# A two-layer hybrid block on one core: strands for casts, subtractions and sums of weights; modulation buffers; new planner costs

## The chip, the cores and the metric

One NeuronCore of one Trainium2 chip runs the whole computation in one launch. The metric is the device time of that launch in microseconds. The engines are called as in the profile: PE (TensorE matmul), PEld (its weight load), DVE (VectorE), ACT (ScalarE), POOL (GpSimd) and SP (SyncE, which here only issues DMAs).

## The reference, cut to what matters

Everything is float32. There are 512 latent tokens and 256 context tokens of 1024 features, and two layers. The context's stream ends inside layer 1, so layer 0 works on 768 tokens and layer 1 on 512 (and on the context's keys and values).

```python
m = silu(cvec) @ w_ada + b_ada                  # 6 x 1024 modulation values, for c and for c_ctx
h = rmsnorm(x, g1) * (1 + sc1) + sh1
z = h @ w_in                                    # 1024 -> 2304: gMLP, gated conv, 2-D Fourier, attention
mix = concat(mixer_a(z), mixer_b(z), mixer_c(z), diff_attention(z))
x = x + gt1 * (mix @ w_out)
h2 = rmsnorm(x, g2) * (1 + sc2) + sh2
up = h2 @ w_up                                  # 1024 -> 2 x 2816
x = x + gt2 * ((silu(dwconv3(up[:2816])) * up[2816:]) @ w_down)
```

The modulation `m` is needed in pieces: `sh1, sc1` before a layer's first projection, `gt2` only when the down projection's results are scaled.

## The kernel before, in words

**Operands.** Features lie on the partitions and tokens on the free axis. A float32 operand is split into a high part (rounded to fp32r by a cast) and a low part (the difference), and each product takes three matmul passes: high by high, high by low, low by high. A weight tile of 128x1024 is loaded into a `wr` buffer by a DMA of SP's queue (4 such buffers), ACT casts it to `wh`, and DVE or POOL subtracts it to `wl` (5 buffers of each). Such a pair is called a unit; the list `plan` fixes their order for the whole program. `load_units` issues the loads, `split_units` makes the units.

**FFN.** The up projection goes by 22 rows f of 128 hidden features, each with an `a` and a `b` half. The first four rows (PLAIN) are plain products with `h2`. From f = 4 on, two rows are taken together as a "quad": seven products on half the tokens in place of eight. For the left factors `split_quad` needs two loaded tiles r0 and r1 and a third buffer rs, four sums of weight pieces (`wr<-wr` on DVE) and four units (.0, .1, .2 of full and .3, `s4h`/`s4l`, of half width). For the right factors `right_factors` builds sums of `h2` blocks once a layer; a last step of it (`hhi<-t`, `hlo<-t`) overwrites halves of `h2`, and can run only when the plain rows have been read. Rows are grouped in chunks (FFN_CHUNKS); the down projection of one chunk comes on PE after the up projection of the next. Each of its eight outputs is scaled by `gt2` on ACT (`ev<-banks,ada`, one instruction a token group) and added to DRAM by a DMA of POOL's queue (`xacc<-ev`); the last chunk alone is added on chip.

**Modulation.** Layer 0's first 40 blocks are made on PE at the start. The other 8 (the `gt2` of layer 0) and the 48 of layer 1 are made by `next_ada` on DVE: one block is a 512 KB load `adaw` by SP's queue and one or two multiply-accumulate instructions over 1024 elements (two where the context needs its own value: blocks 40 to 47 of layer 0 and 0 to 15 of layer 1), then a small add of the bias. It starts when layer 0's mid norm is done. Its two buffers of the pool AR serve for the loaded block and, with two instructions, for the unused product of the first (`junk`).

**The order.** The program is written out by a planner (`Sched`) while it is built. Strands (Python generators) offer instructions; the planner keeps a clock per engine, assumes a duration for each instruction, and always emits the strand that can start first; among those that can start at once it takes the smallest priority number, then the strand that was spawned first. The order in which instructions are emitted is the order in which each engine runs them, and on the chip they wait for one another by semaphores alone. So the assumed durations decide only the order, and the choice of the engine where an instruction may go to several (`("dve", "pool")`). `wl_engine` forces subtractions to POOL in the norm stages and in part of attention. Posts (what follows a product) have priority 1, `split_units` 2, `load_units` 3, `next_ada` 5.

**Lines.** L216 is every plain matmul, L258 every cast or copy on ACT, L261 a copy on DVE, L268 and L270 every two-input elementwise operation on DVE and on POOL, L282 every DVE instruction with a scalar and two tensors, L295 and L297 a scaling on ACT and on POOL, L198 the adding DMA, L189 every other DMA.

Of the kernel before, what the change touches and what calls it, by code (L numbers as in the profile page):

```python
# [29 lines left out]
FFN_CHUNKS = [2] * 9 + [4]  # L30
# [20 lines left out]
SEM = 0.16  # L51
PEM = 0.08
# [25 lines left out]
TAB = 1.1  # L78


class Sched:
# [7 lines left out]
    BW = 320  # L89

    def __init__(self, nc):
        self.nc = nc
        self.T = dict(pe=0.0, act=0.0, dve=0.0, pool=0.0, sp=0.0)
        self.dclk = 0.0
        self.now = 0.0
# [30 lines left out]
    def _ready(self, req):  # L126
        if callable(req):
            return req()
        opts, outs, ins = req
        return min(max(self._deps(o[0], outs, ins) + (PEM if o[0] == "pe" else 0.0), self.T[o[0]]) for o in opts)  # L130

# [28 lines left out]
    def op(self, opts, outs, ins):  # L160

        yield opts, outs, ins
        start = {o[0]: max(self.T[o[0]], self._deps(o[0], outs, ins)) for o in opts}
# [6 lines left out]
        self.T[e] = end  # L170
        self.busy[e] = self.busy.get(e, 0) + cost
# [7 lines left out]
    def dma(self, out, in_, queues=("sp",)):  # L179
        nc = self.nc  # L180
        eng = dict(sp=nc.sync, act=nc.scalar, pool=nc.gpsimd)
        cost = dict(sp=0.6, act=0.7, pool=1.05)
# [4 lines left out]
        for d in sb[0].shape:  # L187
            n *= d
        yield from self.op([(q, cost[q], lambda q=q: eng[q].dma_start(out, in_)) for q in queues], outs, ins)  # L189
        self.dclk = max(self.dclk, self.now) + 4 * n / self.BW / 1e3  # L190
        for o in outs:
            self._note(self.W, o, self.dclk + 2.2, "dma")
        for i in ins:
            self.R[i.tensor.name].append((*span(i)[1:], self.dclk + 2.2, "dma"))

    def dma_add(self, out, in_):

        yield from self.op([("pool", 1.05, lambda: self.nc.gpsimd.dma_start(out, in_, accum_op=ALU.add))], [], [in_])  # L198
# [3 lines left out]
        self.dclk = max(self.dclk, self.now) + 8 * n / self.BW / 1e3  # L202
        self.R[in_.tensor.name].append((*span(in_)[1:], self.dclk + 2.2, "dma"))
# [22 lines left out]
    def trs(self, items, ident):  # L226
# [3 lines left out]
        yield from self.op([("pe", 0.109 * len(items), emit)], [i[0] for i in items], [i[1] for i in items])  # L230

    def _act(self, out, in_, func, bias=None, scale=1.0, accum=None):
        k = {}
        ins = [in_]
        cost = 0.19 + self.n(in_) / 1200
        for key, v in (("bias", bias), ("scale", scale)):
# [3 lines left out]
            if not isinstance(v, float):  # L240
                ins.append(v)
                cost += 0.09
        outs = [out]
        if accum is not None:
            k["accum_out"] = accum
            outs.append(accum)
            cost += 0.28
# [6 lines left out]
    def copy(self, out, in_, eng=("act",)):  # L254
# [4 lines left out]
        if "dve" in eng:  # L259
            fast = in_.space != bass.MemoryType.PSUM  # L260
            opts.append(("dve", 0.09 + n / (1920 if fast else 960), lambda: self.nc.vector.tensor_copy(out, in_)))  # L261
        yield from self.op(opts, [out], [in_])

    def tt(self, out, a, b, op, eng=("dve",)):
        n = self.n(out)
        opts = []
        if "dve" in eng:
            opts.append(("dve", 0.09 + n / 960, lambda: self.nc.vector.tensor_tensor(out, a, b, op=op)))  # L268
# [4 lines left out]
        yield from self.op(opts, [out], [a, b])  # L273
# [1529 lines left out]
```

## Time and profile before

| | |
|---|---|
| three runs | 1571.81, 1567.7, 1562.89 us, median 1567.7 |
| profiled execution, its own time | 1568.05 us |
| its span, first to last instruction | 1566.3 us |
| PE busy | 1457.6 us (93%) |
| DVE busy | 1172.2 us (75%) |
| ACT busy | 751.5 us (48%) |
| POOL busy | 380.6 us (24%) |
| mean granted PE clock | 0.975 |

The stages, by the span's clock: the start and layer 0's projections and mixers to about 350 us, its norms to 400, its FFN to about 890; layer 1's norm and mixers to about 1165, its FFN to about 1530, then the final norm. Busy time of an engine is read beside what ended its idle time: an engine that is 75% busy can still be what PE waits for.

### The profile page before, as it was taken

Reading aid. Unit: us, or ns where it says so; the run is one execution under the profiler, and the core shown is the slowest. Engines: PE = TensorE matmul, PEld = TensorE weight load, DVE = VectorE, ACT = ScalarE, POOL = GpSimd, SP = SyncE. Lnnn points to the kernel's source line nnn. Section 1 sums busy time; section 2 is a strip of 40 time slices with the busy share of each in tenths; the row PEclk is TensorE's granted clock in tenths of the full one; section 3 lists DMA queues with packets and bytes.
Section 4 is the critical chain, followed back from the end, with each engine's and each line's share of the span. In section 5 each row is a group of like instructions: output and inputs, shape, how many; then the busy total and the mean of one; then the engine's idle time right before and its main releaser. Section 6 shows DMA issues by size and latency. Waiting matters only on the chain.

```text
span 1566.3 us, 24259 instructions
## 1 busy us (share of the span) xinstructions
PE 1457.6 (93%) x9312; PEld 1287.5 (82%) x9312; DVE 1172.2 (75%) x1924; ACT 751.5 (48%) x1161; POOL 380.6 (24%) x368
## 2 busy tenths in 40 slices
PE   6989999997979999999999979978989899999987
PEld 4877787886869999999999869766878788888877
DVE  4748578658977777787869487879778777777785
ACT  4435455223535455555445344735334565555552
POOL 0202422107111112211111323343054222222212
PEclk9999999999989999999999989999999999999999
DMA  9564433115165677665566756253441676665635
GB/s 374 155 210 167 135 91 115 41 54 175 54 150 130 179 185 191 150 165 145 150 185 193 215 184 189 101 153 137 141 135 43 147 157 145 163 155 135 153 111 154
DMA packets 79444, 235.45 MB, mean 150 GB/s; under 512 B 10912, under 2 KB 13088, under 8 KB 79200
## 3 DMA queue, kind: packets, MB, share of 16 engines
q1 hardware_dynamic: 50304, 160.72, 30.9%
q0 software_dynamic: 27872, 72.01, 22.2%
q8 instruction: 73, 1.20, 0.3%
q10 hardware_dynamic: 1152, 1.18, 0.2%
q14 instruction: 43, 0.35, 0.1%
HBM read 165.70 MB, written 56.62 MB: 142 GB/s over the span
## 4 chain that ended last, share of the span: by engine, by line
PE 59%; DVE 24%; issue 6%; DMA 5%; ACT 4%; POOL 2%; SPq 0%; DVEq 0%; ACTq 0%; POOLq 0%
PE banks L216 57%; DVE wl L268 4%; DVE hlo L282 2%; DVE wr L268 2%; DVE mx L308 2%; ACT wh L258 1%; DVE ss L268 1%; DVE fy L282 1%; DVE ht L282 1%; DMA stk<-rhi 1%; DVE adaw L282 1%; PE banks L229 1%; DMA adaw<-in_w_adaT 1%; DVE p L282 1%; DVE lo L268 1%
## 5 line engine op out<-in xcount | busy, mean ns | idle before, releaser
L216 PE MATMUL banks<-hhi,wh 128*128 128x512 f32 (+2 forms) x960 | 303.3, 340 | 9.3 <-ACT ev L295 4.6
L258 ACT CAST wh<-wr 128x1024 fp32r<-128x1024 f32 x224 | 233.7, 1046 | 149.6 <-PE banks L216 82.1
L216 PE MATMUL banks<-hlo,wh 128*128 128x512 f32 (+2 forms) x960 | 297.1, 334 | 7.1 <-DVE hlo L282 7.1
L268 DVE TENSOR_TENSOR wl<-wr,wh 128x1024 fp32r<-128x1024 f32 x191 | 237.7, 1249 | 80.2 <-ACT wh L258 79.0
L216 PE MATMUL banks<-hhi,wl 128*128 128x512 f32 (+2 forms) x960 | 294.9, 332 | 0.0
L198 POOL DMA_DIRECT2D xacc<-ev x144 | 125.4, 921 | 333.3 <-ACT ev L295 330.1
L216 PEld LDWEIGHTS banks<-hhi,wh 128*128 128x128 f32 x960 | 174.4, 193 | 34.3 <-issue 14.3
L216 PEld LDWEIGHTS banks<-hlo,wh 128*128 128x128 f32 x960 | 174.8, 193 | 21.8 <-DVE hlo L282 10.3
L216 PEld LDWEIGHTS banks<-hhi,wl 128*128 128x128 f32 x960 | 174.7, 193 | 12.9
L216 PE MATMUL banks<-hi,wh 128*128 128x512 f32 (+1 forms) x560 | 173.6, 352 | 12.1 <-ACT ev L295 6.5
L216 PE MATMUL banks<-lo,wh 128*128 128x512 f32 (+1 forms) x560 | 171.2, 348 | 0.0
L216 PE MATMUL banks<-hi,wl 128*128 128x512 f32 (+1 forms) x560 | 170.8, 347 | 0.0
L295 ACT ACTIVATE ev<-banks,ada 128x512 f32<-128x512 f32 x216 | 123.0, 614 | 60.9 <-PE banks L216 39.2
L270 POOL TENSOR_TENSOR wl<-wr,wh 128x1024 fp32r<-128x1024 f32 (+1 forms) x33 | 81.8, 2477 | 231.5 <-ACT wh L258 225.8
L216 PEld LDWEIGHTS banks<-hi,wh 128*128 128x128 f32 x560 | 96.4, 189 | 31.8 <-ACT ev L295 12.5
L268 DVE TENSOR_TENSOR wr<-wr 128x512 f32<-128x512 f32 x144 | 105.7, 734 | 4.1 <-DMA wr<-in_w_up 3.2
L216 PEld LDWEIGHTS banks<-hi,wl 128*128 128x128 f32 x560 | 96.4, 190 | 14.4
L216 PEld LDWEIGHTS banks<-lo,wh 128*128 128x128 f32 x560 | 96.7, 190 | 12.7
L216 PE MATMUL banks<-th,wh 128*128 128x384 f32 (+1 forms) x288 | 89.9, 312 | 2.8 <-ACT wh L258 2.8
L216 PE MATMUL banks<-th,wl 128*128 128x384 f32 (+1 forms) x288 | 90.0, 313 | 2.4 <-DVE wl L268 2.4
L248 ACT ACTIVATE p<-banks,nm 128x768 f32<-128x768 f32 x64 | 57.6, 900 | 66.5 <-DVE nm L289 30.7
L216 PE MATMUL banks<-tl,wh 128*128 128x384 f32 (+1 forms) x288 | 89.5, 311 | 0.0
(230 smaller groups left out, 3113.2 us busy)
## 6 DMA issues: line engine op xcount, KB each, us to landing
wr<-in_w_up SPq DMA_DIRECT2D x88, 512.0 KB, 4.3
adaw<-in_w_adaT SPq DMA_DIRECT2D x56, 512.0 KB, 5.3
xacc<-ev POOLq DMA_DIRECT2D x72, 384.0 KB, 10.0
wr<-in_w_dn SPq DMA_DIRECT2D x44, 512.0 KB, 5.0
xacc<-ev POOLq DMA_DIRECT2D x72, 256.0 KB, 7.2
adaw<-in_w_ada SPq DMA_DIRECT2D x40, 384.0 KB, 6.7
wr<-in_w_zt SPq DMA_DIRECT2D x24, 512.0 KB, 4.4
wr<-in_w_o SPq DMA_DIRECT2D x16, 512.0 KB, 3.6
```

The source lines that it names most:

```text
L198: yield from self.op([("pool", 1.05, lambda: self.nc.gpsimd.dma_start(out, in_, accum_op=ALU.add))], [], [in_])
L216: self.nc.tensor.matmul(o, l, r, start=a, stop=b, skip_group_check=more)
L229: self.nc.tensor.transpose(o, i, ident)
L248: return ("act", cost, lambda: self.nc.scalar.activation(out, in_, func, **k), func), outs, ins
L258: opts.append(("act", 0.19 + n / 1200, lambda: self.nc.scalar.copy(out, in_)))
L268: opts.append(("dve", 0.09 + n / 960, lambda: self.nc.vector.tensor_tensor(out, a, b, op=op)))
L270: opts.append(("pool", 0.1 + n * 2.25e-3, lambda: self.nc.gpsimd.tensor_tensor(out, a, b, op=op)))
L282: lambda: self.nc.vector.scalar_tensor_tensor(out, a, s, b, op0=op0, op1=op1, **k))], outs, ins)
L295: emit = dict(act=lambda: self.nc.scalar.activation(out, a, AF.Copy, scale=s), dve=lambda: self.nc.vector.tensor_scalar(out, a, s, None, o ...
L308: lambda: self.nc.vector.tensor_reduce(out, in_, axis=AX.X, op=op), [out], [in_])
```

## The change

1. `split_units` only casts now (`high`). Each cast unit is put on a list, and a strand `split_lows` of the same priority makes the subtractions in that order. In a quad the four sums are a strand of their own (`sums`), spawned for each quad at priority 2; casts wait only for the sum that they read.
2. `next_ada` has a fixed `junk` tile, so that the two AR buffers hold loaded blocks only. Layer 1's 48 blocks move to a strand `rest` that is spawned at priority 2 (PADA) when the right factors of layer 0 are done.
3. FFN_CHUNKS goes from nine chunks of 2 and one of 4 to 4, seven of 2, and 4. The four plain rows are then one chunk.
4. The planner assumes other durations, and a lock: DVE operations with two SBUF inputs and all POOL elementwise operations can't overlap in its clocks. No instruction is added for that on the chip. `wl_engine` is as it was; where it forces nothing, the choice between DVE and POOL stays with the planner.

```diff
-FFN_CHUNKS = [2] * 9 + [4]
+FFN_CHUNKS = [4] + [2] * 7 + [4]
-SEM = 0.16
-PEM = 0.08
+SEM = 0.06
+PEM = 0.06
-    BW = 320
+    BW = 390
+    LAT = dict(sp=2.0, act=2.0, pool=3.0)
...
-        start = {o[0]: max(self.T[o[0]], self._deps(o[0], outs, ins)) for o in opts}
+        start = {o[0]: max(self.T[o[0]], self._deps(o[0], outs, ins), self.port if o[0] in lock else 0.0) for o in opts}
...
+        if e in lock:
+            self.port = end
...
-        cost = dict(sp=0.6, act=0.7, pool=1.05)
+        cost = dict(sp=0.36, act=0.4, pool=0.6)
...
-        self.dclk = max(self.dclk, self.now) + 4 * n / self.BW / 1e3
+        e = next(q for q in queues if self.T[q] != t0[q])
+        self.dclk = max(self.dclk, self.T[e]) + 4 * n / self.BW / 1e3
+        t = self.dclk + self.LAT[e]
...
-            opts.append(("dve", 0.09 + n / 960, lambda: self.nc.vector.tensor_tensor(out, a, b, op=op)))
+            opts.append(("dve", 0.15 + n / 960, lambda: self.nc.vector.tensor_tensor(out, a, b, op=op)))
...
+        lock = ("pool",) if PSUM in (a.space, b.space) else ("dve", "pool")
+        yield from self.op(opts, [out], [a, b], lock)
...
+        def high(key, r, c0, n, free=None):
+            if n == 512:
+                hi = yield from S.get("s4h", F32R)
+            else:
                 hi = yield from WHI.get("wh", F32R)
+            yield from K.copy(hi[:, 0:n], r[:, c0:c0 + n], ("act",))
+            lows.append((key, r[:, c0:c0 + n], hi, n, free))
+
+        def split_lows():
+            while True:
+                yield from K.when(lambda: lows)
+                key, src, hi, n, free = lows.pop(0)
...
+                yield from K.tt(lo[:, 0:n], src, hi[:, 0:n], ALU.subtract, wl_engine() or ("dve", "pool"))
+                units[key] = (hi, lo)
...
+            def sums():
+                yield from K.tt(rs[:, 0:512], r1[:, 0:512], r1[:, 512:1024], ALU.add)
+                yield from K.tt(rs[:, 512:1024], rs[:, 0:512], r0[:, 0:512], ALU.add)
+                done.append("12")
+                yield from K.tt(r1[:, 0:512], r0[:, 0:512], r1[:, 0:512], ALU.add)
+                done.append("3")
+                yield from K.when(lambda: key + ".0" in made)
+                yield from K.tt(r0[:, 512:1024], rs[:, 512:1024], r0[:, 512:1024], ALU.add)
+                done.append("4")
+            K.spawn(sums(), 2)
+            yield from high(key + ".0", r0, 0, 1024)
+            yield from K.when(lambda: "12" in done)
+            yield from high(key + ".1", rs, 0, 1024)
...
+                    junk = pool.tile([128, 1024], F32, tag="junk", name="junk")
...
+                    yield from ada_blocks(0, range(40, 48), 2, AR, silu, junk)
                     yield from K.when(lambda: "free" in quad_t)
...
+                    def rest():
+                        yield from ada_blocks(1, range(16), 2, AR, silu, junk)
+                        yield from make_a(1, 0)
+                        yield from ada_blocks(1, range(16, 48), 1, AR, silu, junk)
+                        yield from make_a(1, 1, 1)
...
+                    K.spawn(rest(), PADA)
                 K.spawn(next_ada(), 5)
...
+PADA = 2
```

## Rows read from the trace of the kernel before

**Rows 1.** The page: its span, the chain, two groups, one DMA issue.

```profile
span 1566.3 us, 24259 instructions
...
PE 59%; DVE 24%; issue 6%; DMA 5%; ACT 4%; POOL 2%; SPq 0%; DVEq 0%; ACTq 0%; POOLq 0%
...
L295 ACT ACTIVATE ev<-banks,ada 128x512 f32<-128x512 f32 x216 | 123.0, 614 | 60.9 <-PE banks L216 39.2
...
adaw<-in_w_adaT SPq DMA_DIRECT2D x56, 512.0 KB, 5.3
```

**Rows 2.** Busy time by stage: PE, PEld, DVE, ACT, POOL, then clock and DMA.

```profile
440.00:480.00 40.00, 30.04 (x144) 26.60 (x143) 23.29 (x39) 13.12 (x23) 5.24 (x6) 0.87 0.69 155
480.00:880.00 400.00, 399.26 (x2267) 380.01 (x2266) 306.25 (x467) 203.22 (x299) 70.69 (x78) 1.00 0.66 174
880.00:960.00 80.00, 71.54 (x434) 62.51 (x434) 64.31 (x102) 31.30 (x52) 25.93 (x23) 0.94 0.50 172
960.00:1160.00 200.00, 181.74 (x1128) 148.57 (x1127) 165.11 (x291) 102.52 (x168) 65.53 (x55) 0.97 0.42 136
1220.00:1500.00 280.00, 261.26 (x1759) 238.37 (x1760) 205.67 (x297) 155.49 (x222) 69.56 (x71) 0.98 0.66 147
```

**Rows 3.** What PE waited for from 1220 to 1500 us: total, times, longest.

```profile
PE banks L216 <- ACT wh L258: 10.9, 7, 2.0
PE banks L216 <- DVE wl L268: 5.3, 7, 0.8
PE banks L216 <- DVE fy L268: 3.4, 1, 3.4
```

**Rows 4.** Timeline from 440 to 476 us: start, duration, engine, idle before.

```profile
453.91 1.22 DVE L282 SCALAR_TENSOR_TENSOR junk<-adaw,silu 128x1024 f32<-128x1024 f32 x1 [4.36 <-DMA adaw<-in_w_adaT]
...
456.78 1.05 ACT L295 ACTIVATE ev<-banks,ada 128x512 f32<-128x512 f32 x2 [4.80 <-DVE ada L268]
457.52 0.95 PE L216 MATMUL banks<-hi,wh 128*128 128x512 f32 x2 [3.36 <-ACT ev L295]
...
458.26 1.96 DVE L268 TENSOR_TENSOR hlo<-t,hhi 128x384 fp32r<-128x384 f32 x4 [1.65 <-ACT hhi L258]
...
466.13 0.69 PE L216 MATMUL banks<-hhi,wh 128*128 128x384 f32 x1 [4.62 <-ACT ev L295]
466.62 0.52 PE L216 MATMUL banks<-hlo,wh 128*128 128x384 f32 x1
...
474.00 0.33 PE L216 MATMUL banks<-hlo,wh 128*128 128x384 f32 x1
```

**Rows 5.** Timeline from 1374 to 1382 us, in one quad of layer 1.

```profile
1374.78 2.19 DVE L282 SCALAR_TENSOR_TENSOR fy<-a,vec,fy 128x511 f32<-128x511 f32 x3
...
1378.26 0.68 DVE L268 TENSOR_TENSOR wr<-wr 128x512 f32<-128x512 f32 x1
...
1378.97 1.04 ACT L258 CAST wh<-wr 128x1024 fp32r<-128x1024 f32 x1
...
1380.07 0.51 PE L216 MATMUL banks<-t,wh 128*128 128x256 f32 x2 [1.51 <-ACT wh L258]
```

**Rows 6.** DVE's instructions on the tile adaw, by stretch: busy and count.

```profile
480.00:770.00 290.00, 43.54 (x69) 1.00 0.66 171
...
880.00:960.00 80.00, 9.04 (x14) 0.94 0.50 172
960.00:1160.00 200.00, 20.77 (x34) 0.97 0.42 136
```

**Rows 7.** Instructions on the tile adaw: count, then minimum, median, maximum in ns.

```profile
L282 DVE SCALAR_TENSOR_TENSOR adaw<-adaw,silu x56: 1210/1218/2380, 425.3 to 1144.8; 128x1024 f32<-128x1024 f32 x56
```

**Rows 8.** Timeline from 1003 to 1011 us, with a multiplication on POOL.

```profile
1003.66 1.01 DVE L282 SCALAR_TENSOR_TENSOR p<-p,c 128x768 f32<-128x768 f32 x1
...
1009.65 2.75 POOL L270 TENSOR_TENSOR avq<-av 128x768 f32<-128x768 f32 x2
...
1009.70 2.22 DVE L282 SCALAR_TENSOR_TENSOR p<-p,c 128x768 f32<-128x768 f32 x1 [0.29 <-POOL p L297]
```

More of the change, by code (lines that the diff above doesn't have):

```diff
@@ L94, in __init__ @@
         self.dclk = 0.0
+        self.port = 0.0
         self.now = 0.0
@@ L128, in _ready @@
             return req()
-        opts, outs, ins = req
-        return min(max(self._deps(o[0], outs, ins) + (PEM if o[0] == "pe" else 0.0), self.T[o[0]]) for o in opts)
+        opts, outs, ins, lock = req
+        return min(max(self._deps(o[0], outs, ins) + (PEM if o[0] == "pe" else 0.0), self.T[o[0]],
+                       self.port if o[0] in lock else 0.0) for o in opts)
     def _deps(self, e, outs, ins):
@@ L201, in dma_add @@
             n *= d
-        self.dclk = max(self.dclk, self.now) + 8 * n / self.BW / 1e3
-        self.R[in_.tensor.name].append((*span(in_)[1:], self.dclk + 2.2, "dma"))
+        self.dclk = max(self.dclk, self.T["pool"]) + 8 * n / self.BW / 1e3
+        self.R[in_.tensor.name].append((*span(in_)[1:], self.dclk + 4.0, "dma"))
     @staticmethod
@@ L241, in _act @@
                 ins.append(v)
-                cost += 0.09
+                cost += 0.05
         outs = [out]
@@ L260, in copy @@
             fast = in_.space != bass.MemoryType.PSUM
-            opts.append(("dve", 0.09 + n / (1920 if fast else 960), lambda: self.nc.vector.tensor_copy(out, in_)))
+            opts.append(("dve", 0.15 + n / (1920 if fast else 960), lambda: self.nc.vector.tensor_copy(out, in_)))
         yield from self.op(opts, [out], [in_])
@@ L280, in stt @@
         k = {} if accum is None else {"accum_out": accum}
-        yield from self.op([("dve", 0.09 + self.n(out) / 960,
-                             lambda: self.nc.vector.scalar_tensor_tensor(out, a, s, b, op0=op0, op1=op1, **k))], outs, ins)
+        lock = () if PSUM in (a.space, b.space) else ("dve",)
+        yield from self.op([("dve", (0.15 if isinstance(s, float) else 0.21) + self.n(out) / 960,
+                             lambda: self.nc.vector.scalar_tensor_tensor(out, a, s, b, op0=op0, op1=op1, **k))], outs, ins, lock)
     def ts(self, out, a, s1, s2, op0, op1=None):
@@ L287, in ts @@
         fast = a.space != bass.MemoryType.PSUM
-        yield from self.op([("dve", 0.09 + self.n(out) / (1920 if fast else 960),
+        yield from self.op([("dve", 0.15 + self.n(out) / (1920 if fast else 960),
                              lambda: self.nc.vector.tensor_scalar(out, a, s1, s2, op0=op0, **k))], [out], ins)
@@ L297, in scale @@
                     pool=lambda: self.nc.gpsimd.tensor_scalar(out, a, s, None, op0=ALU.mult))
-        yield from self.op([(e, opts[e], emit[e]) for e in eng], [out], [a, s])
+        yield from self.op([(e, opts[e], emit[e]) for e in eng], [out], [a, s], ("pool",))
     def vec(self, cost, emit, outs, ins):
@@ L548, in wl_engine @@
             return None
+        lows = []
         def split_units():
@@ L614, in ada_blocks @@
                     d = ada[l][:, j, v:v + 1]
-                    junk = w
-                    if v < nv - 1:
-                        junk = yield from AR.get("junk")
-                    yield from K.stt(junk, w, 1.0, silu[:, v, :], ALU.mult, ALU.mult, accum=d)
-                    AR.put(junk)
+                    yield from K.stt(w if v == nv - 1 else junk, w, 1.0, silu[:, v, :], ALU.mult, ALU.mult, accum=d)
+                AR.put(w)
                 d = ada[l][:, j:j + 1, 0:nv]
```

72 lines of the change are left out of this document (30 added, 42 removed).

## The prediction, made before the changed kernel ran

> **What bounds the kernel now.** I read the page first, then the busy times by stage, then what PE waited for stage by stage, and only then short timelines. The chain of waits is 59% PE and 24% DVE in a span of 1566.3 us [rows 1]: no single engine sets the time everywhere, so the gain must be looked for where PE is not dense. The stages say where that is [rows 2]. In layer 0's FFN, 480 to 880 us, PE is busy 399.26 of 400 us: a faster supply of weights is worth nothing there, and DVE's idle 400 - 306.25 = 93.75 us is free room. PE idles 40 - 30.04 = 10.0 us between 440 and 480, at a clock of 0.87; 8.5 us in the norm after 880; 18.3 us in layer 1's mixers, where DVE is busy 165.11 of 200; and 18.7 us in 280 us of layer 1's FFN. Of the last, 10.9 + 5.3 = 16.2 us are waits for a unit's cast or subtraction, and 3.4 us one wait for the hidden rows of the first chunk [rows 3].
>
> **The change part by part.** The sum is made against the profiled execution's own 1568.05 us, 1.75 us more than its span [rows 1] and 0.35 us above the median of the three runs shown.
>
> *First chunk of four rows, and modulation.* At 457.52 and 466.13 PE stands 3.36 and 4.62 us for `ev`; ACT itself waits 4.80 us for the bias sum `ada`, and DVE 4.36 us for the landing of an `adaw` load [rows 4]: the down projection of the first chunk fills the banks before `gt2` is there. After the second stall PE is at the lower clock: a pass of 384 columns shows 0.52 us at 466.62 and 0.33 at 474.00 [rows 4]. PE idle in these 40 us is 10.0; the clock of 0.87 is worth at most 0.13 x 40 = 5.2 us more [rows 2], of which a part falls into the idle time, and I count half. The removed cost is up to 13 us. In the new order the first down projection stands behind the first quad rows, 2 x 84 passes of 384 columns (seven products of four blocks in three passes, for `a` and for `b`; at 2267 passes of all widths in 400 us, 0.176 us each, that is 30 us [rows 2]), while the stalls for `gt2` before end with the one at 466.13 [rows 4]. What is late next is the last step of the right factors, which the down projection covered: four subtractions in 1.96 us [rows 4], and the quad takes them one after the other, so 2 to 3 us show. Net -10 us, bounds -13 and 0. In layer 1 the same move takes away the 3.4 us wait for the hidden rows [rows 3] and uncovers the right factors too, which end there just as the plain rows do: 0, bounds -3 and +3.
>
> The buffers of the modulation by themselves I cost at nothing: before, the next load could already go into the `junk` buffer once the first multiplication was through, and the strand asks for a block only after the last one's instructions are emitted, so loads stay one at a time. Eight evictions of layer 0 in two groups and eight of layer 1 go, 24 of 614 ns [rows 1], 14.7 us of ACT, and 16 adding DMAs: hidden, since ACT is busy 203.22 of 400 and 155.49 of 280 us [rows 2].
>
> *Modulation at priority 2.* After 880 us DVE still spends 9.04 + 20.77 = 29.8 us on `adaw` [rows 6], in the stages where PE waits for DVE. They move before 880 us, where 93.75 us are free: DVE goes there from 306 to 336 of 400 us. In the mixers the gain is at most PE's idle 18.3 us [rows 2], and nothing if PE waits there for something else; with DVE busy 83% and the chain through DVE for 24% of the whole [rows 1, 2], I take half: -9, bounds -18 and 0.
>
> The other side of it: a block is multiplied soon after its load now. The planner counts 0.36 us for the issue, 2.0 us and 512 KB at 390 GB/s, 3.7 us together, and the trace has 5.3 us from issue to landing (median) [rows 1]: 1.6 us in which DVE, which runs its queue in order, may stand with subtractions and posts behind the waiting multiplication, and PE's units behind those. For 48 blocks that is 77 us of DVE at the most, against 64 us that are left idle; so 0 to +13 us for PE. I take +3, near the lower end, because DVE's idle time hides what comes spread out. The Trainium skill's "DMA: Bandwidth & Descriptors" (the cost model's fixed part) has about 2.0 us and the bytes at 436 GB/s, an estimate of 3.2 us for this block. By that the planner would be right and this term 0; the row of 5.3 us disagrees, and decides.
>
> *Casts, subtractions and sums apart.* In a quad of layer 1 the chain reads: three convolution posts `fy` on DVE from 1374.78, then the sum `wr` at 1378.26, the cast at 1378.97, and PE's matmul at 1380.07 after 1.51 us of waiting [rows 5]. The third sum stood behind the second unit's cast and subtraction in one strand, came late to DVE, and found posts ahead. In the new order it can follow the second sum at once, some 4 us earlier, and this wait and the one for the subtraction behind it (5.3/7 = 0.76 us) disappear. They are the 16.2 us of [rows 3], seven of each; a little of the same kind comes after 1500 us. Whether it all goes depends on the loads (two tiles in, one for sums, of four buffers) and on DVE, busy 205.67 of 280 us [rows 2]; at 16 us less it would be busy 78%. I take -12, bounds -19 and 0. Layer 0 gets nothing from it, since PE is dense there.
>
> *Costs and lock.* Nothing of this is an instruction. The trace bears the lock out: `p<-p,c` takes 1.01 us at 1003.66, and 2.22 us at 1009.70 with two POOL multiplications from 1009.65 [rows 8]; an `adaw` multiplication has a median of 1218 ns and a maximum of 2380 [rows 7]. But the forced POOL subtractions stay. What a truer order is worth no row shows: from the nearest, a stretch of 1.2 us [rows 7, 8] won or lost on some seven instructions, I put -8 to +8 and take 0. The Trainium skill's "SBUF — State Buffer" (its reading of the port diagram) says that the shared port pair is an exclusive lock held for a whole instruction. The 2.22 us agree with it: one POOL instruction of about 1.37 us, then the DVE instruction.
>
> Sum: -10 + 0 + 0 - 9 + 3 - 12 + 0 = -28, so 1568.05 - 28 = 1540 us.
>
> **The rivals.**
>
> *Only the start of layer 0's FFN gains.* For it: units need loads, and four `wr` buffers are what they were, so an earlier sum may only move the wait from cast to DMA; and in the mixers PE's wait may pass to the stacks' DMAs and the softmax chain. Against it: the waits of [rows 3] name cast and subtraction, not a DMA. It gives -10 + 3 plus a few either way, 1561 us.
>
> *Slower: modulation crowds out the sums in layer 0's FFN.* The strand `rest` is spawned before the `sums` strands of later quads at the same priority 2, so a ready modulation block goes ahead of a ready sum on DVE. If all of [rows 6]'s later work falls before 770 us, DVE carries 29.8 us and part of the rest more in 290 us than before; at 306.25/400 of 290, 222 us, it comes to some 260, or 90%, before any standing for loads. Should that pass 100% now and then, each of layer 0's 14 quads pays what layer 1's did, 16.2/7 = 2.3 us, 32 us in all, and 13 us of standing for landings come on top: 1568 - 31 + 45 = 1582. Against it: a block's load of 5.3 us comes between two blocks, and in that time the sums, 0.68 us each, find DVE. It decides once DVE is over 95% busy in 480 to 770 us, with PE under 390 of 400.
>
> *More than forecast.* All bounds at their better end: -13 - 3 - 18 - 19 = -53, 1515 us. Little speaks for everything at once.
>
> That the change doesn't do what it says is possible for the lock alone: it may only exchange which engine waits; that is inside the forecast's ±8.
>
> **How the numbers follow.** Forecast 1540 (1522 to 1556): 0.57. Only the start gains, 1561: 0.23, about half of it on either side of the line at 1560. Crowded out, 1582: 0.13, nearly all slower. More than forecast: 0.07. A difference of 0.5%, 7.8 us, is about what a measurement here can tell from none, so faster means under 1559.9 and slower over 1575.5. Faster: 0.57 + 0.11 + 0.07 = 0.75; within: 0.12 + 0.02 = 0.14; slower: 0.11. The range that leaves out 2 in 10 goes from 1512, just under the third rival, to 1573, between the first and the second.
>
> **What would show it.** Right: PE's clock at 1.00 and no wait for `ev` around 450 to 480; no `adaw` on DVE after about 880 and DVE under 150 of 200 us in layer 1's mixers; in layer 1's FFN the waits for `wh` and `wl` together under 6 us; layer 0's FFN still dense. Wrong: PE waiting in layer 0's FFN for `wl` or `wh`, or DVE there idle for `adaw` landings by more than 20 us; in layer 1's FFN the waits under other names (loads `wr`, slots). If the sum holds only because the norms got shorter, the steps are wrong even where the time is right.

## The result and the profile after

The changed kernel takes 1522.62 us, the median of four runs (1519.20 to 1526.69), against 1565.43 us for the kernel before in the same job. The ratio is 0.972, with a 95% interval of 0.968 to 0.977: faster by 2.8%, about 43 us where 28 were forecast. The profiled execution took 1526.69 us, the longest of the four; its span is 41.7 us less than [rows 1].

The page of the changed kernel first. Its lines are numbered a little higher: L216 is L224 now, L258 L266, L268 L276, L282 L292, L295 L305.

```profile
span 1524.6 us, 24194 instructions
...
PE 1449.2 (95%) x9312; PEld 1285.9 (84%) x9312; DVE 1136.3 (75%) x1910; ACT 750.1 (49%) x1165; POOL 330.8 (22%) x336
...
PE 67%; issue 14%; DVE 8%; DMA 5%; POOL 4%; ACT 1%; SPq 1%; POOLq 0%; DVEq 0%; ACTq 0%
...
L305 ACT ACTIVATE ev<-banks,ada 128x512 f32<-128x512 f32 x192 | 111.4, 616 | 78.8 <-PE banks L224 52.1
...
adaw<-in_w_adaT SPq DMA_DIRECT2D x56, 512.0 KB, 5.1
```

DVE's share of the chain falls from 24% in [rows 1] to 8%, while its busy time falls only from 1172.2 to 1136.3 us. It is tempting to read the gain from that share, but the experiments below forbid it: in them the share and the time do not go together. The 24 evictions are gone as forecast, 16 of 512 columns and 8 of 256 (the page's line names only the commonest shape).

To find where the 41.7 us come from I cut each trace at the same five events: the last matmul of the output projection `w_o`, the last matmul of a quad (`th`), the last matmul `hi,wh` of the down projection, each for layer 0 and, without the last, layer 1. The length of each stage is the difference of two such times in the timeline:

| stage (us) | before | after | difference |
|---|---|---|---|
| start to last `w_o`, layer 0 | 359.6 | 350.6 | -9.0 |
| norm, FFN of layer 0 to the last quad | 493.0 | 488.2 | -4.8 |
| to the last down projection, layer 0 | 54.7 | 55.1 | +0.4 |
| norm, projections, mixers of layer 1 to last `w_o` | 253.2 | 241.7 | -11.5 |
| norm, FFN of layer 1 to the last quad | 358.7 | 334.2 | -24.5 |
| last down projections and final norm | 47.1 | 54.9 | +7.8 |

Next the busy times of the changed kernel in stretches that answer to [rows 2]. The columns are the stretch and its length, then PE, PEld, DVE, ACT, POOL, granted PE clock, DMA share, GB/s.

```profile
440.00:480.00 40.00, 40.00 (x230) 37.79 (x229) 33.78 (x51) 18.40 (x24) 1.82 (x2) 1.00 0.50 157
450.00:800.00 350.00, 350.00 (x2005) 333.68 (x2004) 283.66 (x453) 170.33 (x250) 48.62 (x56) 1.00 0.70 182
800.00:840.00 40.00, 35.13 (x184) 33.86 (x183) 36.08 (x58) 17.61 (x22) 0.00 (x0) 0.91 0.53 172
893.90:1135.60 241.70, 226.48 (x1405) 186.79 (x1404) 187.82 (x332) 120.47 (x200) 81.17 (x72) 0.96 0.41 129
1200.50:1469.70 269.20, 267.04 (x1884) 249.13 (x1884) 215.17 (x327) 156.93 (x225) 47.96 (x56) 1.00 0.64 158
```

And the kernel before, cut at the same events of layer 1 (mixers, quads):

```profile
907.30:1160.50 253.20, 229.29 (x1412) 189.73 (x1411) 210.44 (x366) 122.91 (x201) 83.20 (x72) 0.96 0.44 143
1231.90:1519.20 287.30, 266.12 (x1837) 244.74 (x1836) 214.25 (x314) 155.17 (x220) 62.42 (x64) 0.98 0.63 146
```

Two things are to be seen. From 450 to 800 us PE is busy without a gap while DVE is busy 283.66 of 350 us, 81%. And in layer 1's quads PE idles 269.20 - 267.04 = 2.2 us where it idled 21.2, with 47 more matmuls in the stretch. What PE waited for there (total us, times, longest), in the changed kernel:

```profile
PE banks L224 <- DVE wl L276: 2.0, 3, 1.0
```

and in the kernel before, over its own quads:

```profile
PE banks L216 <- ACT wh L258: 11.7, 8, 2.0
PE banks L216 <- DVE wl L268: 7.4, 9, 1.7
```

### The profile page after: what moved, and what is told of

Read it like the earlier page. It is cut to its first block, busy times and chain, and to the rows that moved or that the text cites. A ratio compares the mean times of both kernels' runs of the same rounds, so it can differ in the third digit from the quotient of the medians.

```text
span 1524.6 us, 24194 instructions
## 1 busy us (share of the span) xinstructions
PE 1449.2 (95%) x9312; PEld 1285.9 (84%) x9312; DVE 1136.3 (75%) x1910; ACT 750.1 (49%) x1165; POOL 330.8 (22%) x336
## 4 chain that ended last, share of the span: by engine, by line
PE 67%; issue 14%; DVE 8%; DMA 5%; POOL 4%; ACT 1%; SPq 1%; POOLq 0%; DVEq 0%; ACTq 0%
PE banks L224 66%; POOL xacc L206 3%; PE banks L237 2%; DMA adaw<-in_w_ada 1%; DVE ss L276 1%; DMA adaw<-in_w_adaT 1%; DVE hlo L292 1%; DMA x<-xacc 1%; DVE wl L276 1%; SPq L195 1%; DVE ht L292 1%; DVE p L292 0%; DMA wr<-in_w_o 0%; DMA stk<-rhi 0%; DVE mx L318 0%
## 5 line engine op out<-in xcount | busy, mean ns | idle before, releaser
L266 ACT CAST wh<-wr 128x1024 fp32r<-128x1024 f32 x224 | 233.9, 1048 | 170.4 <-PE banks L224 104.0
L224 PE MATMUL banks<-hlo,wh 128*128 128x512 f32 (+2 forms) x960 | 295.8, 332 | 16.3 <-DVE hlo L292 16.2
L224 PE MATMUL banks<-hhi,wh 128*128 128x512 f32 (+2 forms) x960 | 300.4, 337 | 0.6 <-ACT hhi L256 0.6
L224 PE MATMUL banks<-hhi,wl 128*128 128x512 f32 (+2 forms) x960 | 295.1, 332 | 5.6 <-DVE wl L276 5.6
L276 DVE TENSOR_TENSOR wl<-wr,wh 128x1024 fp32r<-128x1024 f32 x186 | 228.9, 1232 | 65.1 <-ACT wh L266 64.0
L206 POOL DMA_DIRECT2D xacc<-ev x128 | 110.4, 866 | 627.2 <-ACT ev L305 621.9
L224 PEld LDWEIGHTS banks<-hlo,wh 128*128 128x128 f32 x960 | 173.8, 191 | 30.9 <-DVE hlo L292 18.8
L224 PEld LDWEIGHTS banks<-hhi,wh 128*128 128x128 f32 x960 | 173.3, 191 | 22.3 <-issue 9.7
L224 PEld LDWEIGHTS banks<-hhi,wl 128*128 128x128 f32 x960 | 173.5, 191 | 19.8 <-DVE wl L276 6.5
L224 PE MATMUL banks<-hi,wh 128*128 128x512 f32 (+1 forms) x560 | 173.1, 351 | 4.4 <-DVE x L292 3.9
L224 PE MATMUL banks<-lo,wh 128*128 128x512 f32 (+1 forms) x560 | 171.7, 348 | 0.0
L224 PE MATMUL banks<-hi,wl 128*128 128x512 f32 (+1 forms) x560 | 171.6, 348 | 0.0
L278 POOL TENSOR_TENSOR wl<-wr,wh 128x1024 fp32r<-128x1024 f32 (+1 forms) x38 | 93.9, 2474 | 296.1 <-ACT wh L266 259.6
L305 ACT ACTIVATE ev<-banks,ada 128x512 f32<-128x512 f32 x192 | 111.4, 616 | 78.8 <-PE banks L224 52.1
L224 PEld LDWEIGHTS banks<-hi,wh 128*128 128x128 f32 x560 | 97.8, 192 | 18.2 <-DVE x L292 4.1
L224 PEld LDWEIGHTS banks<-hi,wl 128*128 128x128 f32 x560 | 97.4, 192 | 14.1
L224 PEld LDWEIGHTS banks<-lo,wh 128*128 128x128 f32 x560 | 97.7, 192 | 13.5
L276 DVE TENSOR_TENSOR wr<-wr 128x512 f32<-128x512 f32 x144 | 96.2, 686 | 15.0 <-DMA wr<-in_w_up 13.9
L224 PE MATMUL banks<-th,wl 128*128 128x384 f32 (+1 forms) x288 | 89.5, 311 | 2.7 <-DVE wl L276 2.7
L224 PE MATMUL banks<-th,wh 128*128 128x384 f32 (+1 forms) x288 | 89.0, 309 | 1.5 <-ACT wh L266 1.5
L318 DVE TENSOR_REDUCE mx<-banks 128x1 f32<-128x768 f32 (+1 forms) x80 | 67.8, 848 | 30.0 <-PE banks L224 28.1
L292 DVE SCALAR_TENSOR_TENSOR x<-banks,ada,x 128x256 f32<-128x256 f32 (+1 forms) x88 | 49.7, 576 | 53.4 <-PE banks L224 31.6
```

Of the source, the lines that this page charges most:

```text
L206: yield from self.op([("pool", 0.9, lambda: self.nc.gpsimd.dma_start(out, in_, accum_op=ALU.add))], [], [in_])
L224: self.nc.tensor.matmul(o, l, r, start=a, stop=b, skip_group_check=more)
L266: opts.append(("act", 0.19 + n / 1200, lambda: self.nc.scalar.copy(out, in_)))
L276: opts.append(("dve", 0.15 + n / 960, lambda: self.nc.vector.tensor_tensor(out, a, b, op=op)))
L278: opts.append(("pool", 0.1 + n * 2.25e-3, lambda: self.nc.gpsimd.tensor_tensor(out, a, b, op=op)))
L292: lambda: self.nc.vector.scalar_tensor_tensor(out, a, s, b, op0=op0, op1=op1, **k))], outs, ins, lock)
```

## The experiments

Twelve kernels ran, in three jobs, each with the kernel before on the same chip (1568.37, 1567.51 and 1566.86 us in the median). Ratios are to that kernel. Differences from the changed kernel are taken between ratios, times 1565 us. The interval of the changed kernel's ratio alone is 7 us either way, so an experiment's time shows only what is above that, and what is smaller rests on the stages. Those of all runs, cut as above (us):

| | start | FFN 0 | down 0 | mixers 1 | FFN 1 | end |
|---|---|---|---|---|---|---|
| before | 359.6 | 493.0 | 54.7 | 253.2 | 358.7 | 47.1 |
| after | 350.6 | 488.2 | 55.1 | 241.7 | 334.2 | 54.9 |
| u_strands | 350.2 | 485.5 | 60.5 | 233.4 | 366.7 | 52.0 |
| o_strands | 357.8 | 487.6 | 55.5 | 249.7 | 330.4 | 47.6 |
| u_planner | 357.2 | 480.6 | 53.6 | 247.1 | 336.0 | 49.3 |
| o_planner | 351.4 | 502.8 | 58.2 | 238.0 | 367.1 | 52.0 |
| no_lock | 371.6 | 495.5 | 62.4 | 240.2 | 334.4 | 49.8 |
| u_chunks | 349.9 | 502.0 | 54.9 | 226.4 | 332.2 | 54.4 |
| u_ada | 351.0 | 480.7 | 56.0 | 235.4 | 359.6 | 51.9 |
| rest25 | 351.6 | 479.9 | 55.6 | 236.2 | 356.8 | 51.6 |
| pada5 | 351.9 | 480.0 | 55.2 | 238.2 | 357.9 | 52.2 |
| early25 | 349.9 | 482.7 | 55.3 | 237.0 | 345.2 | 53.1 |
| early25_380 | 351.2 | 480.4 | 53.4 | 234.2 | 350.5 | 52.4 |
| nudge | 351.0 | 490.1 | 53.9 | 233.2 | 332.8 | 54.6 |

**u_strands: the changed kernel with the old single strand for casts, subtractions and sums.**

```diff
-            K.spawn(sums(), 2)
-            yield from high(key + ".0", r0, 0, 1024)
...
-            K.spawn(split_lows(), 2)
+            yield from part(0, r0[:, 0:1024], 1024)
+            yield from K.tt(rs[:, 0:512], r1[:, 0:512], r1[:, 512:1024], ALU.add)
...
+            yield from part(3, r0[:, 512:1024], 512)
```

> The changed kernel with the one strand that casts, subtracts and sums in turn put back; chunks, modulation and planner costs as changed. Theory (strands carry layer 1's FFN): the two waits of a quad for wh and wl come back there, 12 to 19 us, the rest stays: about 1538 us. Rival (the truer planner costs carry it): layer 1's FFN stays dense, 1520 to 1526 us.

1554.22 us, ratio 0.9915 (0.9892 to 0.9939): 30 us of the 43 are lost again, 16 us more than expected, and layer 1's FFN is 32.5 us longer. Its quads (busy times as above):

```profile
1200.10:1496.30 296.20, 276.10 (x1886) 254.47 (x1885) 218.74 (x328) 159.22 (x226) 48.61 (x56) 0.98 0.62 144
```

and PE's waits there, with one more from the norm ahead of them:

```profile
PE banks L224 <- DVE wl L276: 10.1, 11, 2.9
PE banks L224 <- ACT wh L266: 7.7, 5, 1.7
...
PE banks L224 <- ACT hhi L256: 6.1, 1, 6.1
```

The last of these is a late modulation block, 12.8 us behind the last `w_o` matmul, of which u_ada tells more. The waits for `wh` and `wl` are back, 17.8 us as expected, but the stretch is 27.0 us longer: PE's idle time grows by 20.1 - 2.2 = 17.9 us, and its busy time by 9.1 us for two more matmuls, at a clock of 0.98 against 1.00. That second part was in no term of the forecast.

**o_strands: the kernel before with the new strands alone.** The diff is that of u_strands, the other way round.

> The kernel before with the strands alone; chunks, modulation and planner costs of before. Theory (the strands by themselves remove the waits for wh and wl in layer 1's FFN): these waits under 6 us there and 12 to 20 us less in all, 1547 to 1556 us. Rival (they need the other costs or an early modulation to pay): 1562 us or more.

1531.82 us, ratio 0.9777 (0.9760 to 0.9794): 35 us faster than the kernel before, alone. That is more than the theory gave. Its quads hold the same 1837 matmuls as those of the kernel before:

```profile
1221.30:1481.00 259.70, 258.04 (x1837) 238.75 (x1836) 212.43 (x305) 155.68 (x221) 69.35 (x67) 1.00 0.66 164
```

287.30 - 259.70 = 27.6 us: idle time from 21.2 to 1.7, which is 19.5, and busy time from 266.12 to 258.04, which is 8.1, with the clock from 0.98 to 1.00. ACT and DVE are as busy as before within 2 us. All that PE still waited for there is

```profile
PE banks L216 <- ACT ev L295: 1.3, 1, 1.3
PE banks L216 <- POOL hlo L270: 0.4, 1, 0.4
```

so no wait for `wh` or `wl` is left, and the loads did not become the wait, as the first rival had it. Which of the two divisions does it, subtractions from casts or sums from both, no run separates. The page's chain names DVE more often than in the changed kernel and less often than before:

```profile
PE 71%; DVE 18%; issue 4%; DMA 3%; ACT 2%; POOL 1%; SPq 0%; DVEq 0%; ACTq 0%; POOLq 0%
```

**u_planner: the changed kernel with the old durations and no lock.**

```diff
-    BW = 390
+    BW = 320
...
-        if e in lock:
-            self.port = end
...
-            opts.append(("dve", 0.15 + n / 960, lambda: self.nc.vector.tensor_tensor(out, a, b, op=op)))
+            opts.append(("dve", 0.09 + n / 960, lambda: self.nc.vector.tensor_tensor(out, a, b, op=op)))
```

> The changed kernel with the old planner durations and without the lock in its clocks; strands, chunks and modulation as changed. Theory (costs and lock are worth nothing by themselves): 1517 to 1529 us. Rival (costs and lock carry the gain that the prediction did not count, the 9 us ahead of layer 0's FFN and part of the mixers of layer 1): 1537 to 1545 us.

1526.81 us, ratio 0.9775 (0.9728 to 0.9823): 4 us slower than the changed kernel by the medians, 8 by the ratios, with intervals that overlap. The stages do differ, by both signs: start +6.6, FFN 0 -7.6, mixers +5.4, end -5.6. DVE's share of its chain is 23%, nearly that of [rows 1].

**o_planner: the kernel before with the new durations and the lock alone.** The diff of u_planner, the other way round.

> The kernel before with the new durations and the lock alone. Theory (an order by truer costs helps little while one strand casts, subtracts and sums in turn): 1555 to 1568 us, the stretch ahead of layer 0's FFN 6 to 9 us shorter, the waits for wh and wl in layer 1's FFN still 12 us or more. Rival (costs and lock carry a large part): 1545 us or less.

1572.73 us, ratio 1.0038 (1.0022 to 1.0053): 6 us slower than the kernel before. The start gains 8.2 us (9.0 in the changed kernel) and the mixers 15.2 (11.5 there); FFN 0 loses 9.8, FFN 1 8.4 and the end 4.9. In FFN 0 PE waits 15.8 us for `ev`, against 9.2 before (400 to 480 us); in the quads of layer 1 the waits for units are as large as before:

```profile
PE banks L224 <- ACT wh L266: 11.0, 7, 1.6
PE banks L224 <- DVE wl L276: 9.7, 10, 2.9
```

Yet DVE's share of the chain is the changed kernel's 8%, in a kernel that is 6 us slower than the one before:

```profile
PE 64%; issue 17%; DVE 8%; DMA 6%; POOL 3%; ACT 1%; SPq 1%; POOLq 0%; DVEq 0%; ACTq 0%
```

So the share goes with the planner's costs and not with the time.

**no_lock: the changed kernel with its new durations, but operations that don't hold the port in the planner's clocks.**

```diff
-        self.port = 0.0
+        self.port = -1.0
...
-        if e in lock:
-            self.port = end
```

> The changed kernel with the lock out of the planner's clocks, the new durations kept. Theory (the lock is worth nothing or little): 1519 to 1528 us. Rival (the lock is what makes DVE's stretched operations fewer, 47 us of them against 73 before): stretched DVE time back to over 65 us and 1530 us or more.

1553.94 us, ratio 0.9915 (0.9888 to 0.9942): 30 us are lost, as the rival had it. The page:

```profile
PE 1456.4 (94%) x9312; PEld 1287.4 (83%) x9312; DVE 1157.1 (74%) x1853; ACT 746.3 (48%) x1160; POOL 445.1 (29%) x401
```

The planner hands POOL 401 - 336 = 65 more instructions than in the changed kernel, 62 of them elementwise, since in its clocks they run beside DVE's. Summed over DVE's instructions that overlap a POOL operation, what they take over the median of the same operation without one is 97 us, against 47 in the changed kernel and 73 before. The Trainium skill's "SBUF — State Buffer" (its two sides) states that a DVE operation with two SBUF inputs and a GpSimd operation that reads SBUF exclude each other for a whole instruction. The sums agree in direction. But this sum doesn't set the time by itself: it is 85 us in u_planner, which plans without a lock too, and 86 us in o_strands, both far faster than this kernel. 21.0 of the loss stand at the start, in this kernel

```profile
0.00:371.60 371.60, 340.59 (x2456) 277.11 (x2457) 232.77 (x445) 166.16 (x285) 83.39 (x73) 0.96 0.45 147
```

and in the changed one:

```profile
0.00:350.60 350.60, 333.68 (x2456) 273.79 (x2457) 218.82 (x445) 168.18 (x286) 68.36 (x64) 0.99 0.44 152
```

The same 2456 matmuls and 445 instructions of DVE, but 15.0 us more of POOL and 14.0 us more of DVE. PE idles 14.1 us more there, and its waits that grew are named for the `adaw` loads of the start (12.3 us against 6.5), for `x` on DVE (4.2 against none) and for a DMA of the stacks (3.5 against 0.8). So most of them name a DMA, not DVE; how they hang on the operations given to POOL is not settled, and the 30 us are those of one order.

**u_chunks: the changed kernel with the old chunks.**

```diff
-FFN_CHUNKS = [4] + [2] * 7 + [4]
+FFN_CHUNKS = [2] * 9 + [4]
```

> The changed kernel with the chunks of before (nine of 2, one of 4). Theory: the stall for gt2 at the start of layer 0's FFN comes back in part, 5 to 10 us, and nothing else: about 1530 us. Rival (the modulation with its own junk tile is early enough by itself): 1520 to 1526 us.

1523.09 us, ratio 0.9731 (0.9701 to 0.9760): nothing in all, as its rival had it. Yet in its place the step does what was forecast. Busy times at the start of layer 0's FFN and in layer 1's mixers:

```profile
440.00:480.00 40.00, 28.20 (x143) 25.62 (x143) 28.85 (x52) 16.46 (x28) 6.11 (x7) 0.87 0.81 208
...
906.70:1133.10 226.40, 219.62 (x1405) 183.69 (x1404) 176.56 (x317) 122.37 (x201) 72.45 (x70) 0.99 0.39 123
```

and PE's wait from 430 to 490 us:

```profile
PE banks L224 <- ACT ev L305: 12.9, 4, 8.9
```

The wait for `ev` is back, PE idles 11.8 us in those 40, and FFN 0 is 13.8 us longer than in the changed kernel. The mixers of the same build are 15.3 us shorter, by PE's idle time, from 15.2 to 6.8, and the clock, from 0.96 to 0.99. The chunks of an FFN don't touch the mixers' code; the order there came out otherwise, and whether it is the modulation (six multiplications on `adaw` are left there in place of twelve) or chance is open.

**u_ada: the changed kernel with the old modulation, its order and its buffers.**

```diff
-                    def rest():
...
-                    K.spawn(rest(), PADA)
+                    yield from ada_blocks(1, range(16), 2, AR, silu)
+                    yield from make_a(1, 0)
+                    yield from ada_blocks(1, range(16, 48), 1, AR, silu)
+                    yield from make_a(1, 1, 1)
```

> The changed kernel with the modulation of before (junk in the two load buffers, layer 1's blocks in the strand of priority 5). Theory (DVE freed in layer 1's mixers): 5 to 9 us come back there, layer 0's last chunk gets 3 to 8 us faster: 1520 to 1530 us, with over 25 us of adaw on DVE after layer 0's FFN. Rival (the freed DVE is the whole of the mixers' gain): about 1534 us.

1537.03 us, ratio 0.9821 (0.9790 to 0.9852): 15 us slower than the changed kernel, by neither of the two mechanisms that I had. FFN 0 is 7.5 us and the mixers 6.3 us *shorter*. The loss is one stall, in the timeline ahead of layer 1's FFN:

```profile
1151.82 1.23 DVE L292 SCALAR_TENSOR_TENSOR adaw<-adaw,silu 128x1024 f32<-128x1024 f32 x1 [1.52 <-DMA adaw<-in_w_adaT]
...
1156.07 1.23 DVE L292 SCALAR_TENSOR_TENSOR adaw<-adaw,silu 128x1024 f32<-128x1024 f32 x1 [2.82 <-DMA adaw<-in_w_adaT]
1157.41 0.16 DVE L292 SCALAR_TENSOR_TENSOR acol<-ada,vec 128x8 f32<-128x8 f32 x1
1158.13 0.91 ACT L256 ACTIVATE hhi<-ht,ada 128x256 fp32r<-128x256 f32 x2 [26.45 <-DVE ht L292]
1158.69 0.58 PE L224 MATMUL banks<-hhi,wh 128*128 128x256 f32 x1 [27.42 <-ACT hhi L256]
```

The last of the 48 modulation blocks is multiplied at 1156.07, 32.8 us after the last `w_o` matmul (1123.3). The strand makes the scaling `acol` of the normed rows only behind it, and ACT and PE stand 26 and 27 us for that. At the old priority the modulation has a date that it misses once everything ahead of it is faster: in the kernel before the last block came at 1144.8, 15.7 us ahead of that matmul.

**rest25 and pada5: priority 2.5 and 5 in place of 2, buffers as changed.**

```diff
-PADA = 2
+PADA = 2.5
```

> The changed kernel with layer 1's modulation strand at priority 2.5 in place of 2, so behind the sums of the quads and ahead of the loads. Theory (in the changed kernel's last chunk of layer 0's FFN, 800 to 815 us, two modulation multiplications go ahead of the sums, and PE waits 4.9 us there and runs at a lower clock after it): that wait goes, layer 0's FFN gets 5 to 8 us shorter, in all 1514 to 1520 us. Rival (the wait is DVE's load in general, or comes back later as a late end of the modulation at layer 1's FFN): 1520 to 1526 us.

> The changed kernel with layer 1's modulation strand at priority 5, the fixed junk tile kept. Theory (the priority is what meets the date at which layer 1's mid norm needs the modulation, not the buffers): as with the old modulation, a stall of some 25 us of PE ahead of layer 1's FFN, 1532 to 1540 us. Rival (two load buffers speed the blocks up by themselves): no such stall, 1518 to 1526 us.

1534.17 and 1534.63 us, ratios 0.9798 (0.9765 to 0.9830) and 0.9793 (0.9766 to 0.9820), 11 to 12 us slower than the changed kernel; for rest25 that is worse than both its expectations. Both have u_ada's stall, here for rest25:

```profile
PE banks L224 <- ACT hhi L256: 26.6, 3, 24.6
```

and for pada5:

```profile
PE banks L224 <- ACT hhi L256: 27.8, 3, 25.8
```

pada5 differs from u_ada by the buffers and by the strand of its own, and is 4 us off, inside the intervals: the buffers are worth nothing that can be told. rest25 shows the other half. FFN 0 is 8.3 us shorter, as the theory had it: priority 2 lets modulation go ahead of the sums in layer 0's last chunk. In the changed kernel:

```profile
806.30 1.21 DVE L292 SCALAR_TENSOR_TENSOR adaw<-adaw,silu 128x1024 f32<-128x1024 f32 x1
...
808.08 1.22 DVE L292 SCALAR_TENSOR_TENSOR adaw<-adaw,silu 128x1024 f32<-128x1024 f32 x1
...
810.10 1.28 DVE L276 TENSOR_TENSOR wr<-wr 128x512 f32<-128x512 f32 x2
...
810.81 1.05 ACT L266 CAST wh<-wr 128x1024 fp32r<-128x1024 f32 x1 [5.63 <-DVE wr L276]
...
811.91 0.81 PE L224 MATMUL banks<-t,wh 128*128 128x384 f32 x2 [2.33 <-ACT wh L266]
```

Two multiplications (with two posts among them, left out here), then the sum, then the cast, for which ACT had stood 5.63 us, then PE after 2.33 us. This is the forecast's second rival, in the last chunk alone, where the rival had priced 14 quads (the layer has 18).

**early25: priority 2.5, with the eight blocks of `gt2` after the scaling of the mid norm, which doesn't need them.** Tried as a version to beat both.

```diff
-                        yield from ada_blocks(1, range(16, 48), 1, AR, silu, junk)
+                        yield from ada_blocks(1, range(16, 40), 1, AR, silu, junk)
                         yield from make_a(1, 1, 1)
+                        yield from ada_blocks(1, range(40, 48), 1, AR, silu, junk)
...
-PADA = 2
+PADA = 2.5
```

> The changed kernel with the modulation strand at priority 2.5 and the scale of layer 1's mid norm made as soon as its block 39 is there, ahead of the eight gate blocks 40 to 47, which only the down projection needs. Theory (the stall of 24.6 us ahead of layer 1's FFN at priority 2.5 is the date of the last block; eight blocks of some 2.6 us go from in front of it): stall under 6 us, layer 0's FFN as short as at 2.5, in all 1511 to 1517 us. Rival (the gate blocks behind it crowd DVE at the start of layer 1's FFN): 1518 to 1528 us.

1520.03 us, ratio 0.9704 (0.9684 to 0.9723), 15 us better than rest25: with eight blocks fewer before the date the stall goes, which makes lateness its cause. The time is the rival's (1518 to 1528), not the theory's. PE's waits from 1120 to 1200 us:

```profile
PE banks L224 <- DVE wl L276: 7.0, 1, 7.0
PE banks L224 <- ACT hhi L256: 2.4, 2, 1.9
```

A single wait of 7.0 us for a subtraction takes part of its place, so FFN 1 remains 11.0 us longer than in the changed kernel, and the whole can't be told from it.

**nudge and early25_380: 2.6% less assumed bandwidth, in the changed kernel and in early25.** Nothing on the chip changes but the order that the planner writes.

```diff
-    BW = 390
+    BW = 380
```

> The changed kernel with one assumed rate of the planner moved by 2.6% (BW 380 in place of 390): the same work in a slightly other order. It measures what any reshuffling is worth. Theory (stages differ by several us between orders that are equally good): within 6 us of the changed kernel, 1517 to 1529 us, with layer 1's mixers moving by over 3 us. Rival (the order is settled, such a nudge changes nothing): within 1.5 us, all stages alike.

> The same with the assumed rate of DMAs at 380 in place of 390. Theory (the gain of the early scale does not hang on one order, though a nudge moved the changed kernel itself by 5 us): 1508 to 1520 us, again without a stall over 6 us ahead of layer 1's FFN. Rival (it was one lucky order): 1524 us or more.

1517.17 us (0.9677, 0.9651 to 0.9704) and 1523.39 us (0.9726, 0.9704 to 0.9749). By the ratios the changed kernel gains 7 us and early25 loses 3, both with intervals that overlap. early25_380 lies between its two expectations, and its longest wait for `hhi` is 6.3 us, so the early scaling keeps the large stall away in a second order too, though not all of it. In nudge it is the mixers, 8.5 us:

```profile
895.10:1128.30 233.20, 222.91 (x1405) 183.74 (x1404) 181.83 (x326) 120.81 (x201) 81.91 (x70) 0.99 0.42 129
```

So a stage can move by 8 us, and the whole perhaps by 3 to 7, with no cause but the order. nudge is the fastest of all by its median; its interval overlaps the changed kernel's, so it is not shown to be faster.

## Why the prediction was right, and which step was not

The direction was right and the range (1512 to 1573) held the time, but 1540 us was 17 us too long, and the sum hides a gain and a cost put too small, a gain right by another mechanism, and two terms that were not there. Those two, -9.0 at the start and +7.8 at the end, nearly cancel, and that is luck.

- **First chunk, -10: right in its place.** PE is busy 40.00 of 40 us from 440 to 480, where it was busy 30.04 [rows 2], at a clock of 1.00, with no wait for `ev` left; u_chunks gives 13.8 us back in this stage, just over the bound of 13. The stage as a whole shows only -4.8, since the modulation takes 7.5 to 8.3 us of it (u_ada, rest25). That u_chunks has the same total as the changed kernel comes from other stages.
- **Strands, -12 (bounds -19 and 0): the mis-sized term.** Alone they are worth 35 us (o_strands), and undone 30 (u_strands). I took the 16.2 us of named waits in [rows 3] as the most that there was, and then less. In the quads alone it is 27.6: the waits between 1220 and 1500 us are not all of the stage, whose idle time is 21.2 us, and 8.1 us of busy time go with them. So the step that failed is taking the named waits as the whole price. I did count the clock at 440 to 480, and left it out here, although [rows 2] shows 0.98 for this stage. By spans o_strands is 37.7 us shorter than the kernel before; the other 10.1 lie outside these quads (FFN 0 -5.4, mixers -3.5, start -1.8, the rest +0.6) and may be order alone. "Layer 0 gets nothing from it" rests on the same dense stretch, and is neither borne out nor refuted by 5.4 us.
- **Modulation earlier, -9 in the mixers: size near, mechanism wrong.** The mixers lost 11.5 us, and DVE 210.44 - 187.82 = 22.6 us of work there. But u_ada, rest25 and early25, which leave more of the modulation to that time than the changed kernel (19.6 us of DVE in each, against 14.7), have mixers of 235 to 237 us, shorter than its 241.7. What the mixers' time goes with is the planner's costs: with the old ones it is 247 to 253 us, with the new ones 226 to 242, o_planner's 238.0 included, which has none of the other steps. DVE's instructions on `adaw` in the changed kernel's mixers and in its layer 0 FFN (stretch, busy time and count, clock, DMA; each multiplication counts as two) are

```profile
893.90:1135.60 241.70, 14.72 (x24) 0.96 0.41 129
...
350.60:838.80 488.20, 78.53 (x128) 0.99 0.60 163
```

  and in the mixers of the kernel before 28.59 us in 44. So only half had moved out of the mixers; "no `adaw` on DVE after about 880" did not come true [rows 6], nor did "under 150 of 200 us" for DVE in the mixers (187.82 of 241.70 is 155 of 200). The half that I took leaned on DVE's 24% of the chain, a share that does not go with the time, as o_planner shows. What the step is worth is something that the forecast doesn't mention: it meets the date of layer 1's mid norm. Without it (u_ada) a stall of 25 to 27 us comes, of which 15 us are left in the whole, since FFN 0 and the mixers are shorter there.
- **Its cost, +3 for standing on landings: too small, and wrong in kind.** What DVE stood for in front of `adaw` multiplications between 350.6 and 838.8 us of the changed kernel (total us, times) is

```profile
  DMA adaw<-in_w_adaT: 2.8, 1
```

  one wait, where I had allowed 1.6 us for each block; five more, 11.7 us together, come later, against 11.0 us in four in the whole of the kernel before. The Trainium skill's "DMA: Bandwidth & Descriptors" (its anatomy of one DMA) gives its fixed part and rate as a fit for DMAs by the GpSimd path, and `adaw` goes by SP's queue, so the 3.2 us taken from it were a loose comparison; the page of the changed kernel has 5.1 us. The 7.5 to 8.3 us that the step costs in FFN 0 are sums queued behind multiplications: the second rival, but only in the last chunk, where DVE is busy 36.08 of 40 us and PE 35.13; in rest25 PE is busy without a gap from 450.0 to 831.5, the end of the quads. From 450 to 800 us, with DVE at 81%, PE lost nothing; the rival had reckoned with 90% there and set its point of decision at 95%.

- **Layer 1's start, 0 within 3: not shown apart, nothing against it.** u_chunks has 2.0 us less in FFN 1 than the changed kernel.
- **Costs and lock, 0 within 8: right for the two together, wrong as one step.** u_planner and the changed kernel are 4 to 8 us apart, o_planner 6 us slower than the kernel before. But new durations without the lock cost 30 us. I had counted the lock as an exchange of which engine waits; in no_lock it also decides how much is given to POOL, though that this makes the loss is not shown.
- **The start, -9, was not forecast.** u_planner has 6.6 us of it back and o_planner alone gains 8.2, so the planner's costs with the lock make it (without the lock the start is 12.0 us longer than before); I had looked for gains in the stages after it only.
- **The end, +7.8, was not forecast either.** The final pass adds to `x`, which has to come back from memory behind the last adding DMAs. DVE stands for that in both kernels, and in the one before longer:

```profile
1538.91 0.48 DVE L282 SCALAR_TENSOR_TENSOR x<-banks,ada,x 128x256 f32<-128x256 f32 x1 [10.03 <-DMA x<-xacc]
```

  and in the changed one

```profile
1488.09 0.48 DVE L292 SCALAR_TENSOR_TENSOR x<-banks,ada,x 128x256 f32<-128x256 f32 x1 [8.65 <-DMA x<-xacc]
1488.63 0.58 PE L224 MATMUL banks<-hi,wh 128*128 128x256 f32 x1 [3.87 <-DVE x L292]
```

  What differs is that PE stands for the same add now, 3.87 us, where it waited 0.4 us for `x` before, and that the clock is lower after it. The whole end, first before and then changed:

```profile
1519.20:1566.30 47.10, 37.31 (x275) 33.93 (x273) 26.76 (x55) 18.40 (x33) 14.16 (x18) 0.94 0.63 160
1469.70:1524.60 54.90, 41.03 (x275) 37.58 (x273) 27.11 (x54) 19.00 (x34) 14.25 (x20) 0.85 0.55 141
```

  For the same 275 matmuls that is 4.1 us more of idle time and 3.7 us more of busy time, at 0.85 against 0.94. In every kernel with the new costs and the lock PE stands 3.0 to 4.2 us at once for `x` there and the end takes 52 to 55 us; with the old costs (before, o_strands, u_planner) or without the lock it stands 1.6 us at a time at most, and the end takes 47 to 50. Why PE has no other work at that moment in these orders, no run tells.

## What to carry to other kernels

Where a chain of load, sum, cast and subtraction is written as one strand, look at the waits between its links, not at the load of the engines: with DVE as busy as before (1176.1 us against 1172.2), giving the links strands of their own took 35 us off. Don't read the gain from an engine's share of a chain of waits: here it was 18% in a kernel 35 us faster and 8% in one 6 us slower. A background job needs a date, not only a priority: it must be checked against the date after each speed-up of what runs ahead of it. And when a planner writes the order, try truer durations together with the resources that engines share (here durations without the lock lost 30 us, in one order), and run its output with one assumption nudged before a few us are put down to an edit.

## What was not expected of the hardware

- Waits of up to 2 us on PE came with a loss beyond their length. For the same 1837 matmuls PE was busy 266.12 us at a mean granted clock of 0.98 and 258.04 at 1.00 (before and o_strands): 8.1 us beside 19.5 us of idle time, about 0.4 us for each us. A clock of 0.98 over 287.3 us accounts for an estimated 5 to 6 us of it; the rest is open, and ends of matmuls are modelled in the profile.
- DVE can be over 80% busy for 350 us with PE never waiting, and 90% busy in 40 us with PE idle 4.9 (changed kernel, 450 to 800 and 800 to 840 us).
- The lock, in one instruction. In the changed kernel a multiplication of 1024 elements, 1218 ns in the median, took 2.92 us once:

```profile
883.53 2.92 DVE L292 SCALAR_TENSOR_TENSOR adaw<-adaw,silu 128x1024 f32<-128x1024 f32 x1
```

  and on POOL stood

```profile
882.98 2.38 POOL L278 TENSOR_TENSOR wl<-wr,wh 128x1024 fp32r<-128x1024 f32 x1 [10.48 <-ACT wh L266]
```

  POOL ends at 885.36, DVE 1.09 us later, at 886.45: 1.09 us is nearly the whole length of such an instruction alone, so it reads as if DVE did its work after POOL's had ended, as in [rows 8]. This happened although the planner kept the two apart in its clocks: the order that it plans holds on the chip, its times don't.
